# Two causal convolutions read TensorE's products in PSUM instead of a copy in SBUF

## The chip, the cores and the metric

The kernel runs on one core of a Trainium2 chip. The metric is the device time of one execution in microseconds (us). Five engines work side by side, each on a queue of its own instructions: TensorE (PE in the profile; PEld are its weight loads), VectorE (DVE), ScalarE (ACT), GpSimd (POOL) and SyncE (SP, which issues transfers). Matmuls write to PSUM, a memory of eight banks of 512 float32 columns in 128 partitions; the other engines read it, and SBUF holds everything else.

## What is computed

One step of one layer of a hybrid decoder, for a prompt of 2048 rows and for 8 sample sequences of 8 rows, with 1024 columns. The lines that matter here, cut from the reference:

```python
def causal_dwconv(x, buf, w):          # x (B,T,C), buf the W-1 rows before, w (W,C)
    width = w.shape[0]
    xp = jnp.concatenate([buf.astype(x.dtype), x], axis=1)
    y = xp[:, 0:t] * w[0]
    for j in range(1, width):
        y = y + xp[:, j:j + t] * w[j]
    return y, xp[:, t:]
...
z = hn @ w_in[i]
qkv, buf_qkv = causal_dwconv(z_qkv, conv_qkv[i], dn_conv_w[i])     # 4 taps, 1536 columns
qkv = jax.nn.silu(qkv).reshape(bsz, t, 3, DN_HEADS, DN_HEAD_DIM)
...                                   # delta rule, S5 and HGRN2 recurrences, output projection
up, buf_ffn = causal_dwconv(hn @ ffn_w_up[i], conv_ffn[i], ffn_conv_w[i])   # 3 taps, 5632 columns
a_ff, b_ff = jnp.split(up, 2, axis=-1)
h = h + (jax.nn.silu(a_ff) * b_ff) @ ffn_w_down[i]
```

So each convolved value is the sum of the products of its own row and of the 3 (or 2) rows before it. The rows before the first are zeros for the prompt and a given state for each sample. The last 3 (or 2) raw rows are outputs.

## The kernel before

**Layout.** The projections are computed transposed: the 128 columns of one weight block stand in the partitions, the rows of the input in the free dimension. The rows are cut into four groups. Groups 0 to 2 have 512 prompt rows each, group 3 has 512 prompt rows and the 64 sample rows, which it computes as two blocks of 320 and 256. Everything is float32 by splitting: an operand is a high part and the rest, and `mm3` issues three matmuls (high by high, high by low, low by high) for each of the 8 slices of 128 input columns, 24 matmuls to a block.

**Phases.** Phase 1 (line 832) is the input projection. It runs over the blocks of `p1_blocks` (line 769: two each of `hq`, `hg`, `u`, `hf`, then the twelve of `qkv`, then four of `zg`), a first pass with groups 0 and 1 and a second pass with groups 2 and 3. Between its blocks stand the small matmuls of the recurrences (delta rule, S5, HGRN2). Phase 3 is the output projection, phase 4 (line 2320) the up-projection over 44 blocks of 128 columns, again first groups 0 and 1, then 2 and 3. Phase 5 is the down-projection, and phase 6 the rest. In this execution the first pass of phase 1 lies at some 160 to 480 us, the second at 480 to 960, and the second pass of phase 4 at 1930 to 2420.

**PSUM.** The blocks of the projections go to the pool `mm` with three banks (line 2696), the small matmuls to the pool `mx` with five (line 2697). A bank can be written again when its last reader is done.

**A convolution unit** is one block of columns of one group. `p1_evac` (line 947) and `p4_evac` (line 2348) make it in these steps. `edges` (line 901, GpSimd) writes the 3 (or 2) columns ahead of the group into the SBUF tile `raw`: zeros, or the tail of the group before (`tail`, `ftail`), and in group 3 the samples' state (`stq`, `fst`) too. `conv_evac` (line 918, ScalarE) reads the bank twice, once unscaled to `raw` and once, scaled by the last tap's weight, to `y`; in group 3 a third copy takes the sample columns apart. From then on the bank is free. `conv` (line 927, VectorE) adds the other taps: for each, one `scalar_tensor_tensor` of 512 columns from `raw`, shifted by a column each time, into `y`, and in group 3 one of 64 sample columns. `keep` (line 937, GpSimd) copies the last columns of `raw` to the tail or, in group 3, to the output tiles `cso` and `fso`. ScalarE then applies silu, and `y` is stored to HBM (in phase 4 after a product with its pair).

**What sets the order.** The program is written once, in the order in which the Python code calls the engines, and each engine runs its instructions in that order. Steps after a matmul are put off: `later(ap, fn, ticks)` (line 787) queues a step, and `tick` (line 773), which the code calls after each slice of a block, issues it when a model (`Pace`, line 44) says that `ap` is ready, or after so many ticks at the latest. `Pace` adds up the modelled durations of each engine; it also knows a port that VectorE and GpSimd share, which operands in PSUM don't use. `tick` then lets the recurrences, which are generators, issue a step whose operands the model calls ready; `late` (line 426) holds them back while the model's queue of VectorE or ScalarE is over 2 us ahead. Weights are split in the background: ScalarE rounds the high part `wh`, and `split` (line 380) gives the subtraction that makes `wl` to VectorE or to GpSimd, whichever the model says is free earlier, with a handicap. So whatever a step costs in the model moves the instructions after it.

All instructions pass through one recording helper, so nearly all rows of the profile say line 71. They are told apart by the names of the tiles.

Of the kernel before, what the change touches and what calls it, by code (L numbers as in the profile page):

```python
# [9 lines left out]
F32 = mybir.dt.float32  # L10
# [9 lines left out]
DM = 1024  # L20
# [461 lines left out]
class Model:  # L482
# [418 lines left out]
    def edges(self, raw, taps, first, tail, rows):  # L901


        nc = self.nc
        k = taps - 1
        if first:
            nc.gpsimd.memset(raw[:, 0:k], 0.0)
        else:
            nc.gpsimd.tensor_copy(raw[:, 0:k], tail)
        if rows is not None:  # L910
            nc.gpsimd.tensor_copy(self.sample_part(raw, taps)[:, :, 0:k], rows)

    @staticmethod
    def sample_part(raw, taps):
        k = taps - 1
        return raw[:, k + 512:k + 512 + NSEQ * (k + ST)].rearrange("p (s t) -> p s t", t=k + ST)

    def conv_evac(self, raw, y, ps, c1, m, taps, w):

        k = taps - 1  # L920
        mp = min(m, 512 - c1)
        self.copy_act(raw[:, k + c1:k + c1 + mp], ps[:, :mp])
        self.copy_act(y[:, c1:c1 + m], ps[:, :m], w[:, k:k + 1])
        if mp < m:
            self.copy_act(self.sample_part(raw, taps)[:, :, k:], ps[:, mp:m].rearrange("p (s t) -> p s t", t=8))

    def conv(self, y, raw, w, taps, n):

        for j in range(taps - 1):
            self.nc.vector.scalar_tensor_tensor(y[:, :512], raw[:, j:j + 512], w[:, j:j + 1], y[:, :512], op0=OP.mult,  # L930
                                                op1=OP.add)
        if n > 512:
            ys, rs = y[:, 512:].rearrange("p (s t) -> p s t", t=8), self.sample_part(raw, taps)
            for j in range(taps - 1):
                self.nc.vector.scalar_tensor_tensor(ys, rs[:, :, j:j + 8], w[:, j:j + 1], ys, op0=OP.mult, op1=OP.add)

    def keep(self, raw, taps, last, tail, out):

        nc = self.nc
        k = taps - 1  # L940
        if last:
            nc.gpsimd.tensor_copy(out[:, 0:k], raw[:, 512:512 + k])
            nc.gpsimd.tensor_copy(out[:, k:].rearrange("p (s t) -> p s t", t=k), self.sample_part(raw, taps)[:, :, 8:])
        else:
            nc.gpsimd.tensor_copy(tail, raw[:, 512:512 + k])
# [1942 lines left out]
```

## Time and profile before

| what | value |
|---|---|
| time, median of 3 runs | 3195.06 us (3188.07 to 3197.48) |
| the profiled execution's own time | 3197.95 us |
| its span in the trace | 3196.2 us |
| mean granted clock of TensorE | 0.983 of full speed |
| TensorE busy | 3057.1 us, 96% |
| VectorE busy | 1893.4 us, 59% |
| ScalarE busy | 1195.7 us, 37% |
| GpSimd busy | 887.5 us, 28% |

The rows further down come from the profile page and from views of the same trace. A group of instructions has one row: line, engine, operation, the output tile, an arrow and the input tiles, the shape (partitions by columns), the number of instructions, their busy time and mean in ns, and then the time that the engine stood idle just ahead of them, with what ended most of it. The waits name who waited, for which engine's instruction on which tile, the time in all, how often, and the longest. The granted clock (PEclk) is TensorE's clock as the throttle gave it, as a share of full speed.

### The profile page before, as it was taken

Reading aid. Unit: us, or ns where it says so; the run is one execution under the profiler, and the core shown is the slowest. Engines: PE = TensorE matmul, PEld = TensorE weight load, DVE = VectorE, ACT = ScalarE, POOL = GpSimd, SP = SyncE. Lnnn points to the kernel's source line nnn. Section 1 sums busy time; section 2 is a strip of 40 time slices with the busy share of each in tenths; the row PEclk is TensorE's granted clock in tenths of the full one; section 3 lists DMA queues with packets and bytes.
Section 4 is the critical chain, followed back from the end, with each engine's and each line's share of the span. In section 5 each row is a group of like instructions: output and inputs, shape, how many; then the busy total and the mean of one; then the engine's idle time right before and its main releaser. Section 6 shows DMA issues by size and latency. Waiting matters only on the chain.

```text
span 3196.2 us, 49509 instructions
## 1 busy us (share of the span) xinstructions
PE 3057.1 (96%) x17872; PEld 2533.0 (79%) x17872; DVE 1893.4 (59%) x4208; ACT 1195.7 (37%) x2821; POOL 887.5 (28%) x1303
## 2 busy tenths in 40 slices
PE   6999989999998799999999999999999999999998
PEld 5767778878886677777777889998998888888886
DVE  8566975579696676777555456445444324323655
ACT  5343453443442444433324334333333213223332
POOL 3332423434243232533244225233231001000111
PEclk8999999999999899999999999999999999999999
DMA  6433496453656555344534333222216445444221
GB/s 187 110 112 93 123 261 170 121 155 85 195 148 200 154 160 143 120 118 133 132 89 115 114 108 116 65 71 72 65 51 190 131 124 169 132 134 131 80 79 57
DMA packets 576845, 400.32 MB, mean 125 GB/s; under 512 B 111077, under 2 KB 503145, under 8 KB 576328
## 3 DMA queue, kind: packets, MB, share of 16 engines
q1 hardware_dynamic: 545656, 359.07, 39.8%
q10 hardware_dynamic: 30944, 38.09, 3.4%
q8 instruction: 141, 2.31, 0.3%
q14 instruction: 104, 0.85, 0.1%
HBM read 277.52 MB, written 118.95 MB: 124 GB/s over the span
## 4 chain that ended last, share of the span: by engine, by line
PE 72%; DVE 15%; issue 4%; DMA 3%; ACT 3%; POOL 2%; SPq 1%; ACTq 0%; POOLq 0%; DVEq 0%
PE mm L71 61%; PE mx L71 11%; DVE y L71 3%; DVE rs L71 3%; DVE b L71 2%; DVE s5v L71 1%; DVE R L71 1%; SPq L71 1%; DVE dsc L71 1%; ACT djunk L71 1%; POOL wl L71 1%; ACT y L71 1%; DVE nx L71 0%; DMA Q<-dNN 0%; DMA h<-h 0%
## 5 line engine op out<-in xcount | busy, mean ns | idle before, releaser
L71 PE MATMUL mm<-hnl,wh 128*128 128x512 f32 (+2 forms) x2720 | 985.1, 362 | 8.8 <-DVE hnl L71 8.8
L71 PE MATMUL mm<-hnh,wl 128*128 128x512 f32 (+2 forms) x2720 | 980.6, 360 | 0.0
L71 PE MATMUL mm<-hnh,wh 128*128 128x512 f32 (+2 forms) x2720 | 978.7, 360 | 1.9 <-ACT y L71 1.6
L71 DVE SCALAR_TENSOR_TENSOR y<-raw,fw,y 128x512 f32<-128x512 f32 (+1 forms) x440 | 387.3, 888 | 395.1 <-ACT y L71 290.5
L71 PEld LDWEIGHTS mm<-hnl,wh 128*128 128x128 f32 x2720 | 516.1, 190 | 83.6 <-DVE hnl L71 9.3
L71 PEld LDWEIGHTS mm<-hnh,wh 128*128 128x128 f32 x2720 | 515.8, 190 | 76.9 <-issue 4.9
L71 PEld LDWEIGHTS mm<-hnh,wl 128*128 128x128 f32 x2720 | 516.2, 190 | 72.3 <-issue 3.0
L71 POOL TENSOR_TENSOR wl<-wr,wh 128x512 fp32r<-128x512 f32 (+1 forms) x291 | 410.9, 1420 | 519.6 <-ACT wh L71 466.0
L71 ACT ACTIVATE raw<-mm 128x512 f32<-128x512 f32 (+3 forms) x336 | 155.5, 463 | 415.3 <-PE mm L71 399.9
L71 PE MATMUL mm<-kh,ghi 128*128 128x512 f32 x748 | 294.7, 394 | 0.3 <-ACT ghi L71 0.3
L71 PE MATMUL mm<-kl,ghi 128*128 128x512 f32 x748 | 294.1, 393 | 0.0
L71 PE MATMUL mm<-kh,glo 128*128 128x512 f32 x704 | 277.1, 394 | 0.0
L71 ACT ACTIVATE wh<-wr 128x512 fp32r<-128x512 f32 (+1 forms) x338 | 204.3, 632 | 116.5 <-PE mm L71 53.2
L71 ACT ACTIVATE y<-y 128x512 f32<-128x512 f32 (+1 forms) x136 | 87.8, 645 | 367.6 <-DVE y L71 367.4
L71 ACT ACTIVATE ghi<-kr 128x512 fp32r<-128x512 f32 (+1 forms) x192 | 99.0, 580 | 329.7 <-PE mm L71 281.9
L71 DVE SCALAR_TENSOR_TENSOR y<-raw,cw,y 128x512 f32<-128x512 f32 (+1 forms) x180 | 156.2, 873 | 62.1 <-ACT y L71 28.3
L71 DVE TENSOR_TENSOR h<-mm,h 128x512 f32<-128x512 f32 (+1 forms) x36 | 24.8, 690 | 278.1 <-PE mm L71 278.0
L71 PEld LDWEIGHTS mm<-kh,ghi 128*128 128x128 f32 x748 | 140.6, 188 | 32.5 <-ACT ghi L71 0.7
L71 PEld LDWEIGHTS mm<-kl,ghi 128*128 128x128 f32 x748 | 140.6, 188 | 32.2 <-DVE kl L71 0.6
L71 POOL COPY ftail<-raw 128x2 f32<-128x2 f32 x132 | 31.5, 238 | 468.0 <-ACT raw L71 461.2
L71 PEld LDWEIGHTS mm<-kh,glo 128*128 128x128 f32 x704 | 132.2, 188 | 30.0 <-DVE glo L71 0.4
L71 ACT ACTIVATE y<-mm,fw 128x512 f32<-128x512 f32 (+2 forms) x220 | 133.7, 608 | 12.9 <-DVE y L71 12.0
(525 smaller groups left out, 4691.3 us busy)
## 6 DMA issues: line engine op xcount, KB each, us to landing
wr<-in_ffn_w_up SPq DMA_DIRECT2D x176, 256.0 KB
kr<-gT SPq DMA_DIRECT2D x155, 256.0 KB
wr<-in_w_in SPq DMA_DIRECT2D x112, 256.0 KB
gT<-y SPq DMA_DIRECT2D x66, 256.0 KB
h<-h SPq DMA_DIRECT2D x65, 256.0 KB
Q<-zq SPq DMA_DIRECT2D x32, 512.0 KB
wr<-oT SPq DMA_DIRECT2D x48, 256.0 KB
kr<-in_ffn_w_down SPq DMA_DIRECT2D x44, 256.0 KB
```

The source lines that it names most:

```text
L71: return f(*a, **k)
```

## The change

The tile `raw` is gone, and with it `edges`, `conv` and `keep`. ScalarE still writes `y`, scaled by the last tap, and then copies only the last 3 (or 2) columns of the bank, as the tail for the group behind; that tail has two slots now, by the parity of the group. In group 3 the tail between its two blocks goes to a small tile `ct`, and the last columns of the prompt and of each sample go straight to `cso` or `fso`. VectorE adds the other taps from the bank itself, block by block, so that group 3 has adds of some 318 and some 190 columns and of the samples' 5 to 7 rows out of eight. The first columns of a block lack the rows ahead of it; short adds from the tail (or the state) repair them. The conv step is put off by 9 ticks in phase 1 and 6 in phase 4. Two other users of `raw`'s memory take tiles `nx` instead (the fourth pair of phase 3, the state rows in `ffn_state`). The matmuls, their number and the pools of PSUM are as before.

```diff
@@ conv_evac, conv, keep, edges
-    def edges(self, raw, taps, first, tail, rows):
...
-        nc = self.nc
-        k = taps - 1
-        if first:
-            nc.gpsimd.memset(raw[:, 0:k], 0.0)
-        else:
-            nc.gpsimd.tensor_copy(raw[:, 0:k], tail)
-        if rows is not None:
-            nc.gpsimd.tensor_copy(self.sample_part(raw, taps)[:, :, 0:k], rows)
...
+    def conv_evac(self, y, ps, c1, m, taps, w, tail, rows, last, out):
...
         k = taps - 1
         mp = min(m, 512 - c1)
-        self.copy_act(raw[:, k + c1:k + c1 + mp], ps[:, :mp])
         self.copy_act(y[:, c1:c1 + m], ps[:, :m], w[:, k:k + 1])
+        self.copy_act(out[:, 0:k], ps[:, mp - k:mp])
         if mp < m:
-            self.copy_act(self.sample_part(raw, taps)[:, :, k:], ps[:, mp:m].rearrange("p (s t) -> p s t", t=8))
-
-    def conv(self, y, raw, w, taps, n):
-
-        for j in range(taps - 1):
-            self.nc.vector.scalar_tensor_tensor(y[:, :512], raw[:, j:j + 512], w[:, j:j + 1], y[:, :512], op0=OP.mult,
-                                                op1=OP.add)
...
-    def keep(self, raw, taps, last, tail, out):
...
+            self.copy_act(out[:, k:].rearrange("p (s t) -> p s t", t=k), self.by_seq(ps[:, mp:m])[:, :, ST - k:])
+
+        def add(o, i, j):
+            nc.vector.scalar_tensor_tensor(o, i, w[:, j:j + 1], o, op0=OP.mult, op1=OP.add)
+
+        def conv():
+            for j in range(k):
+                add(y[:, c1 + k - j:c1 + mp], ps[:, :mp - k + j], j)
+            if mp < m:
+                ys, xs = self.by_seq(y[:, 512:512 + NS]), self.by_seq(ps[:, mp:m])
+                for j in range(k):
+                    add(ys[:, :, k - j:], xs[:, :, :ST - k + j], j)
+                for j in range(k):
+                    add(ys[:, :, :k - j], rows[:, :, j:], j)
+            if tail is not None:
+                for j in range(k):
+                    add(y[:, c1:c1 + k - j], tail[:, j:k], j)
+
+        return conv
+
+    def conv_block(self, y, ps, c1, m, n, taps, w, g, tail, rows, out):
+
+        last = c1 + m == n
+        if c1 == 0:
+            self.before = None if g == 0 else tail[:, (g - 1) % 2]
+        to = (out if g == 3 else tail[:, g % 2]) if last else self.sm.tile([128, 3], F32, tag="ct", name="ct")
+        conv = self.conv_evac(y, ps, c1, m, taps, w, self.before, rows, last, to)
+        self.before = to
+        return conv
 
@@ p1_evac
-            if kind == "qkv":
-                self.raw = self.cv.tile([128, 3 + 512 + NSEQ * 11], F32, tag="raw", name="raw")
-                self.edges(self.raw, 4, g == 0, self.tail[:, b],
-                           self.stq[:, b].rearrange("p (s t) -> p s t", t=3) if g == 3 else None)
...
-            self.conv_evac(self.raw, y, ps, c1, m, 4, self.cw[:, b])
+            conv = self.conv_block(y, ps, c1, m, n, 4, self.cw[:, b], g, self.tail[:, b],
+                                   self.stq[:, b].rearrange("p (s t) -> p s t", t=3), self.cso[:, b])
+
+            def rest():
+                conv()
+                if c1 + m == n:
+                    self.p1_finish(g, kind, b, y)
+
+            self.later(y, rest, 9)
+            return
...
-            self.later(self.raw, conv, 12)
+            self.later(y, silu, 9)
@@ phase3, pair
-            if t < 2:
+            if t != 2:
                 return halves(self.np_.tile([128, DM], F32, tag="nx", name="h1x", bufs=self.NX))
-            if t == 2:
-                self.h1y = i
-            return tuple(y_tile() if t == 2 else half_tile("raw", 3 + 512 + NSEQ * 11, 2) for _ in range(2))
+            self.h1y = i
+            return y_tile(), y_tile()
@@ ffn_consts, ffn_state, and the same for tail in phase 1
-        self.ftail = cp.tile([128, 44, 2], F32, name="ftail")
+        self.ftail = cp.tile([128, 44, 2, 2], F32, name="ftail")
...
-            sr = self.cv.tile([128, 3 + 512 + NSEQ * 11], F32, tag="raw", name="fs_rows")[:16, :512]
+            sr = self.np_.tile([128, DM], F32, tag="nx", name="fs_rows", bufs=self.NX)[:16, :512]
@@ p4_evac
-            self.raw = self.cv.tile([128, 3 + 512 + NSEQ * 11], F32, tag="raw", name="raw")
...
-        raw, y = self.raw, self.y
-        self.conv_evac(raw, y, ps, c1, m, 3, self.fw[:, b])
+        y = self.y
+        block = self.conv_block(y, ps, c1, m, n, 3, self.fw[:, b], g, self.ftail[:, b],
+                                self.fst[:, b].rearrange("p (s t) -> p s t", t=2) if g == 3 else None,
+                                self.fso[:, b] if g == 3 else None)
...
-            self.conv(y, raw, self.fw[:, b], 3, n)
-            self.keep(raw, 3, g == 3, self.ftail[:, b], self.fso[:, b] if g == 3 else None)
+            block()
+            if c1 + m < n:
+                return
...
-        if c1 + m == n:
-            self.later(raw, conv, 9)
+        self.later(y, conv, 6)
```

The step that is put off moves the instructions behind it. Three places follow, without the numbers of the rows. In them `y<-mm,cw,y` is an add out of the bank with a weight of the convolution, `s5t`, `s5v`, `la` and `lbm` belong to the S5 scan, `hw`, `hm` to HGRN2, `R` and `V` to the delta rule; a number behind a name is a buffer's.

VectorE in the first pass of phase 1, the end of a run of serial S5 steps and the convolution unit behind it, before:

```order
L71 TENSOR_TENSOR s5t<-b_3025,lbm 128x16
L71 TENSOR_TENSOR b_3025<-s5v,s5t 128x16
L71 TENSOR_TENSOR b_3025<-b_3025,s5t 128x8 x2
L71 SCALAR_TENSOR_TENSOR y<-raw,cw,y 128x512 x3
L71 TENSOR_TENSOR s5t<-b_3025,la 128x16
```

and after:

```order
L71 TENSOR_TENSOR s5t<-b_2992,lbm 128x16
L71 TENSOR_TENSOR b_2992<-s5v,s5t 128x16
L71 TENSOR_TENSOR b_2992<-b_2992,s5t 128x8 x2
L71 SCALAR_TENSOR_TENSOR y<-mm,cw,y 128x509
L71 SCALAR_TENSOR_TENSOR y<-mm,cw,y 128x510
L71 SCALAR_TENSOR_TENSOR y<-mm,cw,y 128x511
L71 SCALAR_TENSOR_TENSOR y<-tail,cw,y 128x3
L71 SCALAR_TENSOR_TENSOR y<-tail,cw,y 128x2
L71 SCALAR_TENSOR_TENSOR y<-tail,cw,y 128x1
L71 TENSOR_TENSOR s5t<-b_2992,la 128x16
```

Eight S5 steps of five instructions stand ahead of the adds in both orders; the adds are now six instead of three, and read the bank.

VectorE in the second pass of phase 1, a unit of group 3 (the delta rule's and HGRN2's instructions around it), before:

```order
L71 TENSOR_TENSOR hw<-hw,b_7920 128x8x32
L71 COPY_PREDICATED b_7919<-hm,mx 32x4x32 x4
L71 SCALAR_TENSOR_TENSOR y<-raw,cw,y 128x512 x3
L71 SCALAR_TENSOR_TENSOR y<-raw,cw,y 128x64 x3
L71 SCALAR_TENSOR_TENSOR R_8667<-mx,d_neg,V 128x128 x4
```

and after, the second of its two blocks:

```order
L71 SCALAR_TENSOR_TENSOR y<-mm,cw,y 128x189
L71 SCALAR_TENSOR_TENSOR y<-mm,cw,y 128x190
L71 SCALAR_TENSOR_TENSOR y<-mm,cw,y 128x191
L71 SCALAR_TENSOR_TENSOR y<-mm,cw,y 128x8x5
L71 SCALAR_TENSOR_TENSOR y<-mm,cw,y 128x8x6
L71 SCALAR_TENSOR_TENSOR y<-mm,cw,y 128x8x7
L71 SCALAR_TENSOR_TENSOR y<-stq,cw,y 128x8x3
L71 SCALAR_TENSOR_TENSOR y<-stq,cw,y 128x8x2
L71 SCALAR_TENSOR_TENSOR y<-stq,cw,y 128x8
L71 SCALAR_TENSOR_TENSOR y<-ct,cw,y 128x3
L71 SCALAR_TENSOR_TENSOR y<-ct,cw,y 128x2
L71 SCALAR_TENSOR_TENSOR y<-ct,cw,y 128x1
```

Six adds of the unit are now eighteen: these twelve, and ahead of them six of the first block (317 to 319 columns, and the repairs of 3, 2 and 1).

GpSimd at the end of phase 1 (`SQ` belongs to the delta rule), before:

```order
L71 TENSOR_TENSOR wl<-wr,wh 128x512 x2
L71 TENSOR_TENSOR SQ<-O,ofac 128x512
L71 COPY raw<-tail 128x3
L71 COPY raw<-stq 128x8x3
L71 COPY cso<-raw 128x3
L71 COPY cso<-raw 128x24
L71 TENSOR_TENSOR wl<-wr,wh 128x512
```

and after:

```order
L71 TENSOR_TENSOR b_9025<-b_8875,hfac 128x512
L71 TENSOR_TENSOR wl<-wr,wh 128x512
L71 TENSOR_TENSOR SQ<-O,ofac 128x512
L71 TENSOR_TENSOR wl<-wr,wh 128x512 x2
L71 TENSOR_TENSOR SQ<-O,ofac 128x512
```

The copies into and out of `raw` are gone, and the splits `wl` stand closer together. Over the whole program `wl` splits of 512 columns go from 44 to 9 on VectorE and from 276 to 311 on GpSimd.

## Rows read from the trace of the kernel before

**Rows 1.** The page, part 1: engine, busy us, share of the span, instructions.
```profile
PE 3057.1 (96%) x17872; PEld 2533.0 (79%) x17872; DVE 1893.4 (59%) x4208; ACT 1195.7 (37%) x2821; POOL 887.5 (28%) x1303
```

**Rows 2.** Busy time by stretches; the first line names the columns.
```profile
core 0: us, PE busy (x) PEld busy (x) DVE busy (x) ACT busy (x) POOL busy (x), PEclk, DMA share, GB/s
...
160.00:480.00 320.00, 294.18 (x1859) 236.33 (x1858) 240.67 (x617) 143.64 (x343) 102.47 (x138) 0.97 0.50 147
480.00:960.00 480.00, 454.92 (x3872) 394.83 (x3870) 346.83 (x889) 204.36 (x580) 180.37 (x223) 0.97 0.52 145
960.00:1100.00 140.00, 110.73 (x493) 87.94 (x494) 99.64 (x249) 46.34 (x123) 47.59 (x38) 0.91 0.60 180
1100.00:1600.00 500.00, 479.48 (x3060) 379.52 (x3060) 343.97 (x794) 208.81 (x546) 168.11 (x275) 0.98 0.49 135
...
1930.00:2420.00 490.00, 490.00 (x2991) 446.58 (x2990) 241.74 (x318) 187.12 (x419) 159.71 (x313) 1.00 0.23 71
```

**Rows 3.** TensorE's waits, 160 to 1600 us: waiter, releaser, us, times, longest.
```profile
PE mx L71 <- DVE d_g L71: 15.3, 4, 6.0
...
PE mx L71 <- POOL raw L71: 5.1, 3, 3.4
...
PE mm L71 <- ACT y L71: 3.8, 2, 2.3
...
PE mx L71 <- POOL A L71: 0.3, 1, 0.3
```

**Rows 4.** ScalarE: costliest groups (busy, mean ns, idle before); a tile's instructions (min/median/max).
```profile
L71 ACT ACTIVATE raw<-mm 128x512 f32<-128x512 f32 (+3 forms) x336 | 155.5, 463 | 415.3 <-PE mm L71 399.9
...
L71 ACT ACTIVATE ba<-mm x17: 158/172/188, 25.2 to 952.0; 128x8 f32<-128x8 f32 x16, 64x8 f32<-64x8 f32 x1
```

**Rows 5.** Groups of GpSimd and VectorE, each shape apart; columns as there.
```profile
L71 POOL TENSOR_TENSOR wl<-wr,wh 128x512 fp32r<-128x512 f32 x276 | 390.3, 1422 | 465.5 <-ACT wh L71 430.1 <-DMA b<-xs 15.9 <-ACT d_egc L71 11.3
...
L71 POOL COPY ftail<-raw 128x2 f32<-128x2 f32 x132 | 31.5, 238 | 468.0 <-ACT raw L71 461.2 <-DVE R L71 3.0 <-DMA A<-dA 2.0
...
L71 DVE TENSOR_TENSOR wl<-wr,wh 128x512 fp32r<-128x512 f32 x44 | 32.4, 737 | 13.5 <-ACT wh L71 13.3 <-issue 0.2
```

**Rows 6.** Groups of VectorE: two of the page, then four with shapes apart.
```profile
L71 DVE SCALAR_TENSOR_TENSOR y<-raw,fw,y 128x512 f32<-128x512 f32 (+1 forms) x440 | 387.3, 888 | 395.1 <-ACT y L71 290.5
...
L71 DVE SCALAR_TENSOR_TENSOR y<-raw,cw,y 128x512 f32<-128x512 f32 (+1 forms) x180 | 156.2, 873 | 62.1 <-ACT y L71 28.3
...
L71 DVE SCALAR_TENSOR_TENSOR SH<-SH,b,mx 64x64 f32<-64x64 f32 x128 | 35.8, 279 | 29.3 <-PE mx L71 26.1
...
L71 DVE SCALAR_TENSOR_TENSOR R<-mx,d_neg,V 128x128 f32<-128x128 f32 x64 | 18.0, 343 | 26.8 <-PE mx L71 26.8
...
L71 DVE SCALAR_TENSOR_TENSOR ZG<-mx,gdn,ZG 128x512 f32<-128x512 f32 x16 | 12.0, 748 | 17.3 <-PE mx L71 14.0 <-DMA A<-dA 3.3
...
L71 DVE SCALAR_TENSOR_TENSOR nrs<-rs 128x1 f32<-128x1 f32 x64 | 10.2, 160 | 2.2
```

**Rows 7.** One group of VectorE, shapes apart, in 480 to 960 us.
```profile
L71 DVE SCALAR_TENSOR_TENSOR y<-raw,cw,y 128x512 f32<-128x512 f32 x72 | 72.2, 1003 | 17.2 <-POOL raw L71 4.7 <-ACT y L71 4.2 <-POOL tail L71 3.4
```

**Rows 8.** The instructions of the tiles `raw` and `hnh`: min/median/max ns, from when, shapes.
```profile
L71 DVE SCALAR_TENSOR_TENSOR y<-raw,fw,y x440: 271/752/3448, 1100.0 to 2421.2; 128x512 f32<-128x512 f32 x104, 128x64 f32<-128x64 f32 x43
...
L71 DVE TENSOR_TENSOR hnl<-mx,hnh x68: 416/683/692, 16.4 to 1909.1; 128x512 fp32r<-128x512 f32 x64, 128x256 fp32r<-128x256 f32 x4
```

**Rows 9.** VectorE's waits, 160 to 1600 us, columns as in Rows 3.
```profile
DVE y L71 <- ACT y L71: 67.2, 27, 9.2
...
DVE y L71 <- POOL ftail L71: 29.7, 8, 9.4
...
DVE y L71 <- POOL raw L71: 18.4, 9, 3.6
```

**Rows 10.** Start and length, us: the chain that ended last; timelines of ScalarE, VectorE.
```profile
1668.76 39.97 PE mm L71 x171
...
343.16 0.60 ACT L71 ACTIVATE raw<-mm 128x512 f32<-128x512 f32 x1 [0.46 <-ACT y L71]
...
354.75 2.32 DVE L71 SCALAR_TENSOR_TENSOR y<-raw,cw,y 128x512 f32<-128x512 f32 x3
```

More of the change, by code (lines that the diff above doesn't have):

```diff
@@ L927, in conv @@
-    def conv(self, y, raw, w, taps, n):
-        for j in range(taps - 1):
-            self.nc.vector.scalar_tensor_tensor(y[:, :512], raw[:, j:j + 512], w[:, j:j + 1], y[:, :512], op0=OP.mult,
-                                                op1=OP.add)
[L932 to L935, printed above, removed]
@@ L937, in keep @@
-    def keep(self, raw, taps, last, tail, out):
-        nc = self.nc
[L940 to L945, printed above, removed]
+            self.copy_act(out[:, k:].rearrange("p (s t) -> p s t", t=k), self.by_seq(ps[:, mp:m])[:, :, ST - k:])
+        def add(o, i, j):
+            nc.vector.scalar_tensor_tensor(o, i, w[:, j:j + 1], o, op0=OP.mult, op1=OP.add)
@@ L987, in out @@
             self.flags.add((kind, b, g))
-        def conv(raw=self.raw if kind == "qkv" else None):
-            self.conv(y, raw, self.cw[:, b], 4, n)
-            self.keep(raw, 4, g == 3, self.tail[:, b], self.cso[:, b])
-            self.later(y, silu, 9)
         def silu():
@@ L2210, in phase3 @@
         both = units[0][0] == units[1][0]
[L2211 to L2212 removed]
+        y_tile = lambda: self.cv.tile([128, 512 + NS], F32, tag="y", name="xh", bufs=3)[:, :512]
         turn = 3 if both else 4
@@ L2355, in p4_evac @@
                 self.need(("hn2", self.h1y))
-            self.raw = self.cv.tile([128, 3 + 512 + NSEQ * 11], F32, tag="raw", name="raw")
             self.y = self.cv.tile([128, 512 + NS], F32, tag="y", name="y", bufs=3)
-            self.edges(self.raw, 3, g == 0, self.ftail[:, b],
-                       self.fst[:, b].rearrange("p (s t) -> p s t", t=2) if g == 3 else None)
-        raw, y = self.raw, self.y
-        self.conv_evac(raw, y, ps, c1, m, 3, self.fw[:, b])
+        y = self.y
+        block = self.conv_block(y, ps, c1, m, n, 3, self.fw[:, b], g, self.ftail[:, b],
+                                self.fst[:, b].rearrange("p (s t) -> p s t", t=2) if g == 3 else None,
+                                self.fso[:, b] if g == 3 else None)
         def conv():
-            self.conv(y, raw, self.fw[:, b], 3, n)
-            self.keep(raw, 3, g == 3, self.ftail[:, b], self.fso[:, b] if g == 3 else None)
+            block()
+            if c1 + m < n:
+                return
             if x == 0:
@@ L2619, in setup_small @@
         self.stq = cp.tile([128, 12, 24], F32, name="stq")
-        self.tail = cp.tile([128, 12, 3], F32, name="tail")
+        self.tail = cp.tile([128, 12, 2, 3], F32, name="tail")
         self.cso = self.cp.tile([128, 12, 27], F32, name="cso")
```

10 lines of the change are left out of this document (3 added, 7 removed).

## Prediction, made before the changed kernel ran

> **What bounds the kernel now.** I read the page's busy times first. TensorE is busy for 96% of the span [rows 1], so an edit that issues no matmul can only pay where TensorE waits. The table by stretches tells where that is. From 1930 to 2420 us, the second pass of the up-projection, TensorE is busy for 490.00 of 490 us at a granted clock of 1.00. It waits in the first half: 25.82 us idle from 160 to 480, 25.08 from 480 to 960, 29.27 from 960 to 1100, 20.52 from 1100 to 1600. That is 100.7 us of 1440, with a granted clock of 0.97, 0.97, 0.91 and 0.98 [rows 2]. If a clock of 0.91 means that 9% of the stretch's matmul rate is missing, the clock costs up to 47 us more there (9.6 + 14.4 + 12.6 + 10.0).
>
> The waits of TensorE in 160 to 1600 us say for whom. There are 25 rows, the first and the last shown, and they add up to 100.6 us: 45.1 for VectorE, 21.3 for ScalarE, 13.2 for GpSimd, 21.0 for transfers. Nearly all are `mx`, the small matmuls of the recurrences that stand in TensorE's order between the blocks of the projection. The projection itself (`mm`) waits for a bank only for 3.8 us [rows 3]. So the convolution is not on the path now. It matters in two ways: it occupies the queues of VectorE, ScalarE and GpSimd that feed the small matmuls, and after the change it also holds the bank.
>
> **The change, part by part.** The program lists the same 15,709 matmuls and transposes before and after. The small ones stand a few blocks earlier or later, and I cost that at nothing by itself.
>
> ScalarE. The 336 copies `raw<-mm` go, 155.5 us. In their place come 280 copies of 2 or 3 columns and 56 of 16 or 24. The nearest row is the 128x8 copy `ba<-mm` at 0.172 us [rows 4], so 336 x 0.172 = 58 us; if each cost what a whole `raw<-mm` costs (0.463), nothing would be gained. I take 58: 97 us off a queue of 1195.7 us, all of it beside matmuls.
>
> GpSimd. All 504 copies into and out of `raw` go; at the mean of the cheapest of their rows, 0.238, that is 120 us. Against that, 35 weight splits `wl` of 512 columns go from VectorE to GpSimd in the new order (44 to 9, and 276 to 311): 35 x 1.422 = 50 us more there and 35 x 0.737 = 26 us less on VectorE [rows 5]. GpSimd ends some 70 us lighter.
>
> VectorE. Removed: 387.3 + 156.2 = 543.5 us. Added are 372 adds of about 510 columns out of PSUM, 124 of about 318, 124 of about 190, 124 of 40 to 56 for the samples, and 620 of one to 24 columns out of SBUF, which repair the first columns. The row with just the operands of the large ones (PSUM, a scalar by partition, SBUF) is `ZG<-mx,gdn,ZG`, 0.748 for 512 columns; `R<-mx,d_neg,V` has 0.343 for 128. The line between them gives 0.543 for 318 and 0.408 for 190; the samples cost about `SH<-SH,b,mx`, 0.279 for 64. A repair lies between `nrs<-rs`, 0.160 for one column, and 0.279, and I take 0.20, nearer to the first [rows 6]. The sum is 372 x 0.748 + 124 x (0.543 + 0.408 + 0.279) + 620 x 0.20 = 278 + 153 + 124 = 555 us (530 to 604). With the splits that left, VectorE changes by 555 - 543.5 - 26 = -14 us (-39 to +35).
>
> It is unevenly spread. A unit is one block of 128 output columns over one group of rows. In 480 to 960 us, where the last group brings the samples along, the twelve pairs of units cost 72.2 us for the 512-column adds and 36 x 0.279 = 10 for the samples before, and 36 x 0.748 + 36 x (0.543 + 0.408 + 0.279) + 144 x 0.20 = 100 us after: +18 us on 346.83 that VectorE is busy there [rows 2, 7]. In 1100 to 1600 us, where the first groups have no or two repairs, it falls.
>
> What goes besides is waiting. An add out of `raw` takes 0.752 us as a rule and up to 3.448 while GpSimd works; the subtraction `hnl<-mx,hnh`, which reads PSUM, stays between 0.416 and 0.692 over 68 instructions [rows 8]. So the large adds lose their tail (mean 0.888 and 0.873 over all forms), and the repairs, with SBUF on both sides, keep one. VectorE's 48.1 us of waiting for GpSimd's `ftail` and `raw` copies (29.7 + 18.4) in 160 to 1600 us goes altogether [rows 9].
>
> On the path: TensorE's 5.1 us of waiting for GpSimd's `raw` copies goes. VectorE's queue gets shorter by about 48 of the 1031 us that it is busy in 160 to 1600, 5%; I take 5% off the other 74.5 us that TensorE waits for the three engines, 4 us. Together -9 us. After 1600 us there is nothing to gain, and I take 0 (0 to +5).
>
> The added wait. A bank of `mm` now comes free after VectorE's last add instead of ScalarE's second copy, and there are three such banks. What is queued behind a late one is the next-but-two block of matmuls, so TensorE itself. A block of 24 matmuls of 512 columns takes 24 x 39.97 / 171 = 5.6 us, so the adds must end 11.2 us after the block. Three adds at 0.752 are 2.3 us, so a unit that meets an empty queue is far inside. The worst is in a row: ScalarE reads the bank at 343.16, and the three adds stand behind the serial S5 steps until 354.75 + 2.32 = 357.07 us, 13.9 us later [rows 10]. In the new order the adds of such a unit still stand behind eight of these steps. I take 3 us for this one and nothing for the rest.
>
> The Trainium skill speaks against this change. "VectorE: DVE Perf Modes", in its rules for kernel authors, says to accept the plain rate out of PSUM or to copy to SBUF first if many operations follow, and its errata section puts the fixed part at 120 cycles out of PSUM against 58. At the page's 0.96 GHz that would be an estimated 65 ns for each of 744 adds, 48 us more on VectorE; that would take back the 4 us of its shorter queue, and the sum below would be 3194 instead of 3190. The rows disagree: 0.748 out of PSUM and a median of 0.752 out of SBUF [rows 6, 8].
>
> The sum: the profiled execution took 3197.95 us (span 3196.2); 3197.95 - 9 + 3 = 3192. The median of the three runs shown, 3195.06, lies 2.9 lower, so I forecast 3190.
>
> **The rivals.** *The queues pay more.* VectorE alone waited 67.2 us for ScalarE's `y` in 160 to 1600 us [rows 9], and the raw copy that stood ahead of each `y` is gone. If a third of the 79.6 us that TensorE waits for the three engines goes, that is 27 us and 3168. For it: 97 and 70 us leave the two side queues. Against it: a chain of small matmuls waits for its own last step, whatever the load.
>
> *The banks decide: slower.* Place: 480 to 960 us, where a block of 512 is followed by one of 320 and one of 256 columns, 576 x 5.6 / 512 = 6.3 us for both, and where VectorE gets 18 us more to do. There an add chain that ends over 6.3 us after its block stops TensorE. If the backlog grows by 3 us in each of the twelve units, about half of that shows: 12 x 1.5 = 18, with 5 us in the first pass 23 us, so 3213. It decides from the point where adds end later than two blocks after their own. For it: 343 to 357 us shows 14 us behind an end of a block. Against it: 3.8 us of bank waits now, and the planner keeps its recurrences back when VectorE is more than 2 us behind.
>
> *The change doesn't do what it says.* GpSimd's freed time goes into the 35 splits, and the wait for ScalarE only moves: 3195.
>
> **How the numbers follow.** About 0.3% (9.6 us) is what a measurement of this kernel can tell from no change. The forecast gets 0.38 and the last rival 0.07, both within it but for 0.03 below; the queues pay more 0.31; the banks 0.24, of which 0.01 stays within. So faster 0.34, same 0.43, slower 0.23. The range 3166 to 3214 reaches to the middle of both rivals on the outside, 3168 and 3213, which leaves about 0.1 out on each side.
>
> **What would show it.** No `raw` row; ScalarE near 1100 and GpSimd near 810 us busy; the 510-column adds at 0.75 with no tail. TensorE busy throughout from 1930 to 2420. Its waits for `DVE y` at `mm` stay under 10 us in all: if they pass 20, the banks decided. If the idle of TensorE from 160 to 1600 falls under 80 us, the queues paid more. I am wrong altogether if the time after 1600 us moves by more than 5 us.

## The result, and the profile after

The changed kernel takes 3215.04 us (median of 5 runs, 3207.5 to 3222.19) against 3195.06 us before. The ratio is 1.0062, with a 95% interval of 1.0045 to 1.0078. So it is slower, by about 20 us, and above the range that I gave (3166 to 3214). The profiled execution took 3215.56 us, its span is 3213.8.

The busy times of the changed kernel, to be read beside [rows 1]:

```profile
PE 3066.5 (95%) x17872; PEld 2539.5 (79%) x17872; DVE 1958.6 (61%) x4911; ACT 1093.2 (34%) x2818; POOL 755.8 (24%) x784
```

ScalarE fell by 102.5 us and GpSimd by 131.7, both more than forecast. VectorE did not fall by 14 us; it rose by 65.2.

The stretches of [rows 2], after, with the same columns:

```profile
160.00:480.00 320.00, 290.63 (x1835) 233.91 (x1834) 240.30 (x653) 130.02 (x334) 91.65 (x95) 0.97 0.49 143
480.00:960.00 480.00, 446.77 (x3773) 386.19 (x3771) 337.93 (x944) 177.50 (x544) 136.53 (x143) 0.96 0.49 138
960.00:1100.00 140.00, 117.18 (x544) 95.12 (x543) 112.06 (x318) 51.54 (x133) 56.68 (x43) 0.91 0.55 167
1100.00:1600.00 500.00, 480.89 (x3080) 380.68 (x3078) 346.69 (x891) 189.54 (x571) 141.69 (x152) 0.98 0.50 141
...
1930.00:2420.00 490.00, 489.60 (x2973) 445.36 (x2972) 304.18 (x713) 152.81 (x424) 112.73 (x88) 1.00 0.23 72
```

In 480 to 960 us TensorE is busy for 446.77 us instead of 454.92. In the second pass of the up-projection it is as full as before, although VectorE works 62 us more there (304.18 against 241.74). That work is covered.

A fixed point of the program shows when the time is lost. The first matmul of the output projection (`mm<-woh,wh`) follows phase 1, the first of the down-projection (`mm<-kh,ghi`) follows phase 4. The instructions of the tiles, before and then after (min/median/max ns, first and last start in us):

```profile
L71 PE MATMUL mm<-woh,wh x128: 388/394/793, 951.5 to 1078.9; 128*128 128x512 f32 x128
L71 PE MATMUL mm<-kh,ghi x748: 387/392/497, 2417.3 to 2932.4; 128*128 128x512 f32 x187
```

```profile
L71 PE MATMUL mm<-woh,wh x128: 387/394/775, 969.5 to 1098.8; 128*128 128x512 f32 x128
L71 PE MATMUL mm<-kh,ghi x748: 387/392/639, 2429.1 to 2947.6; 128*128 128x512 f32 x187
```

The output projection begins 18.0 us later. By the down-projection 6.2 of them are back, and 5.8 more are lost behind it, 17.6 in all.

Cut at these two points, the program shows what the 17.6 us are made of (columns as in [rows 2], before and then after):

```profile
0.00:951.50 951.50, 874.62 (x6333) 734.32 (x6334) 689.91 (x1806) 409.10 (x1036) 331.69 (x439) 0.97 0.51 146
951.50:2417.30 1465.80, 1415.18 (x8111) 1177.93 (x8110) 867.32 (x1663) 563.62 (x1318) 489.92 (x813) 0.98 0.39 112
2417.30:3196.20 778.90, 767.26 (x3432) 620.77 (x3430) 336.19 (x741) 222.96 (x467) 65.94 (x51) 1.00 0.43 125
```

```profile
0.00:969.50 969.50, 879.32 (x6314) 737.14 (x6315) 698.03 (x1954) 381.44 (x1016) 284.96 (x320) 0.96 0.50 143
969.50:2429.10 1459.60, 1417.77 (x8132) 1180.46 (x8131) 927.34 (x2215) 489.18 (x1336) 403.59 (x414) 0.98 0.38 113
2429.10:3213.80 784.70, 769.45 (x3432) 621.90 (x3430) 333.22 (x744) 222.63 (x467) 67.29 (x50) 0.99 0.41 124
```

TensorE issues the same 17872 instructions. It is idle for 8.2 us more (147.3 against 139.1) and busy for 9.4 us more. So only half of the loss is waiting; the other half is the same matmuls at a lower granted clock, 0.980 over the whole span instead of 0.983, and 0.003 of 3214 us is 9.6. Up to the output projection it is 13.3 us of idle time and 4.7 of busy time.

### The profile page after: what moved, and what is told of

It is laid out like the page before. It is cut to its first block, busy times and chain, and to the rows that moved or that the text cites. A ratio compares the mean times of both kernels' runs of the same rounds, so it can differ in the third digit from the quotient of the medians.

```text
span 3213.8 us, 49643 instructions
## 1 busy us (share of the span) xinstructions
PE 3066.5 (95%) x17872; PEld 2539.5 (79%) x17872; DVE 1958.6 (61%) x4911; ACT 1093.2 (34%) x2818; POOL 755.8 (24%) x784
## 4 chain that ended last, share of the span: by engine, by line
PE 57%; DVE 13%; DMA 4%; issue 3%; ACT 1%; POOL 1%; SPq 0%; ACTq 0%; POOLq 0%; DVEq 0%
PE mm L71 49%; PE mx L71 7%; DVE y L71 4%; DVE R L71 3%; DVE rs L71 1%; DVE b L71 1%; DMA h<-h 1%; DVE s5v L71 1%; DMA wr<-oT 1%; DVE dsc L71 0%; DMA t<-dTU 0%; SPq L71 0%; ACT y L71 0%; DMA Q<-dNN 0%; DMA b<-us 0%
## 5 line engine op out<-in xcount | busy, mean ns | idle before, releaser
L71 POOL TENSOR_TENSOR wl<-wr,wh 128x512 fp32r<-128x512 f32 (+1 forms) x327 | 430.7, 1331 | 1205.9 <-ACT wh L71 1138.9
L71 DVE SCALAR_TENSOR_TENSOR y<-mm,fw,y 128x510 f32<-128x510 f32 (+7 forms) x528 | 302.3, 579 | 306.6 <-ACT ftail L71 222.1
L71 DVE SCALAR_TENSOR_TENSOR y<-mm,cw,y 128x511 f32<-128x511 f32 (+8 forms) x216 | 123.9, 578 | 43.5 <-ACT tail L71 31.7
L71 POOL TENSOR_TENSOR kl<-kr,kh 128x512 fp32r<-128x512 f32 x12 | 16.7, 1398 | 449.6 <-ACT kh L71 440.3
L71 PE MATMUL mx<-b,b 64*64 64x64 f32 (+7 forms) x752 | 108.5, 290 | 11.3 <-DMA b<-us 7.9
```

What stands on the lines that cost most here:

```text
L71: return f(*a, **k)
```

## What VectorE did in place of the forecast

VectorE's groups in the changed kernel, each shape apart (count, busy us, mean ns, idle before):

```profile
L71 DVE SCALAR_TENSOR_TENSOR y<-mm,fw,y 128x510 f32<-128x510 f32 x132 | 98.5, 747 | 224.6 <-ACT ftail L71 222.1 <-DMA gT<-y 2.3
...
L71 DVE SCALAR_TENSOR_TENSOR y<-ftail,fw,y 128x1 f32<-128x1 f32 x132 | 55.6, 421 | 4.7
...
L71 DVE SCALAR_TENSOR_TENSOR y<-fst,fw,y 128x8 f32<-128x8 f32 x44 | 29.1, 662 | 1.6
...
L71 DVE SCALAR_TENSOR_TENSOR y<-ct,fw,y 128x2 f32<-128x2 f32 x44 | 9.3, 212 | 0.0
```

The large adds cost just what the sum took: 0.747 us, 278 us for the 372. The middle ones and the samples' come to 153 us, as forecast. The 620 repairs cost 227 us instead of 124, a mean of 0.366 instead of 0.20. By itself that would have made VectorE 89 us busier (103 - 14); some of its other instructions became shorter, such as the product `y<-y` of 512 columns, 0.704 us instead of 0.822. The repairs' median is low, but there is a tail (the tile `ftail`, changed kernel):

```profile
L71 DVE SCALAR_TENSOR_TENSOR y<-ftail,fw,y x264: 219/221/2357, 1154.5 to 2428.6; 128x2 f32<-128x2 f32 x132
```

A place in the second pass of phase 1 shows where the tail is from. VectorE's timeline, and GpSimd's for the same time (start, length in us):

```profile
787.21 0.73 DVE L71 SCALAR_TENSOR_TENSOR y<-tail,cw,y 128x3 f32<-128x3 f32 x3
787.86 2.09 DVE L71 SCALAR_TENSOR_TENSOR y<-mm,cw,y 128x189 f32<-128x189 f32 x6
789.98 1.32 DVE L71 SCALAR_TENSOR_TENSOR y<-stq,cw,y 128x24 f32<-128x24 f32 x3
791.23 1.15 DVE L71 SCALAR_TENSOR_TENSOR y<-ct,cw,y 128x3 f32<-128x3 f32 x3
792.29 0.91 DVE L71 TENSOR_TENSOR R<-Q,R 128x392 f32<-128x392 f32 x1
```

```profile
790.42 0.85 POOL L71 TENSOR_TENSOR hw<-hw 128x256 f32<-128x256 f32 x1 [3.98 <-PE mx L71]
791.24 0.61 POOL L71 TENSOR_TENSOR b<-hw 128x256 f32<-128x256 f32 x1
```

Three repairs take 0.73 us while GpSimd is idle, and 1.32 and 1.15 while it works. Over the whole trace, the 188 repairs that overlap a busy GpSimd instruction of over 0.1 us have a mean of 0.70 us, and the 432 others 0.22, at most 0.245. The Trainium skill ("SBUF — State Buffer", Terms) calls this the shared port pair, held for the full instruction, on which the loser fully blocks. The rows agree: the three repairs from `stq` end at 791.30 us, GpSimd's first instruction at 791.27.

Around this place VectorE is the path. The chain of waits of the changed kernel in 730 to 830 us, by line; below it the same line of the kernel before:

```profile
by line: DVE y L71 56.4%; DVE R L71 21.1%; issue 11.2%; DVE hw L71 2.5%; ACT y L71 2.3%; DVE b L71 2.0%; DVE rs L71 1.7%; DVE SH L71 1.1%; ACT Q L71 1.1%; ACT tail L71 0.6%; DVE hfac L71 0.2%; ACTq L71 0.1%; DVEq L71 0.1%
```

```profile
by line: PE mm L71 27.6%; DVE y L71 21.1%; PE mx L71 17.9%; DVE R L71 8.3%; issue 7.3%; DVE rs L71 3.4%; ACT y L71 2.9%; DVE hw L71 2.4%; ACT raw L71 2.2%; DMA zq<-y 2.1%; POOL wl L71 1.3%; ACT Q L71 1.2%; POOL cso L71 0.7%; ACT wh L71 0.5%
```

TensorE's matmuls had 46% of it (27.6 + 17.9) and have none. And TensorE now waits for VectorE at the bank (three of its waits in 160 to 1600 us; all of them add up to 104.0 us against 100.6 before):

```profile
PE mx L71 <- DVE d_g L71: 15.4, 3, 11.3
PE mm L71 <- DVE y L71: 14.9, 8, 4.4
PE mx L71 <- DVE b L71: 7.9, 3, 5.5
```

Of these 14.9 us, 9.8 lie between 740 and 815 us, where blocks of 320 and 256 columns follow each other. Two stretches with their clocks (columns as in [rows 2]), before and then after:

```profile
740.00:815.00 75.00, 68.48 (x597) 59.73 (x596) 67.56 (x120) 26.93 (x63) 36.70 (x53) 0.95 0.43 120
815.00:860.00 45.00, 44.53 (x411) 38.30 (x409) 26.30 (x81) 20.96 (x78) 7.73 (x12) 1.00 0.68 196
```

```profile
740.00:815.00 75.00, 65.17 (x425) 57.81 (x424) 66.40 (x162) 18.13 (x49) 17.72 (x17) 0.95 0.27 84
815.00:860.00 45.00, 38.82 (x355) 31.10 (x353) 26.83 (x77) 13.58 (x37) 9.59 (x14) 0.84 0.57 159
```

VectorE was already busy for 90% of 740 to 815 us before the change. TensorE is idle for 9.8 us there now (6.5 before), and in the 45 us that follow its granted clock is 0.84, between its two levels (1.00 is 2.4 GHz, 0.50 is 1.2 GHz), where it was 1.00.

## The experiments

Three theories stood against each other. *Repairs*: their 227 us lengthen VectorE's queue, and the small matmuls of the recurrences wait behind it. *Banks*: TensorE waits for a bank that VectorE still reads. *Order*: the recurrences stand in other places, and 35 splits moved to GpSimd; that costs it. All ratios are against the kernel before on the same chip, with 95% intervals.

**Order and work apart.** In x_order the planning model notes the changed kernel's instructions (`nc.note`), while the engines get those of the kernel before (`real`):

```diff
+        nc.note(nc.scalar, "activation", (out[:, 0:k], ps[:, mp - k:mp], AF.Copy), {})
...
+            nc.note(nc.vector, "scalar_tensor_tensor", (o, i, w[:, j:j + 1], o), {})
...
+        act, dve, pool = nc.scalar.real, nc.vector.real, nc.gpsimd.real
...
+        act.activation(raw[:, k + c1:k + c1 + mp], ps[:, :mp], AF.Copy)
...
+                dve.scalar_tensor_tensor(y[:, :512], raw[:, j:j + 512], w[:, j:j + 1], y[:, :512], op0=OP.mult, op1=OP.add)
```

> The convolution is made as in the kernel before (raw copies on ScalarE, adds out of SBUF, edges and keeps on GpSimd), but the model that sets the order is fed the changed kernel's instructions, so that TensorE's order, the places of the steps and the engine of each weight split are those of the changed kernel. Theory 'order' (the recurrences' new places and the 35 moved splits cost the 20 us): 3211 to 3220. Theories 'banks' and 'repairs' (the work itself costs it): 3190 to 3200, the time of the kernel before.

Measured: 3213.54 us, ratio 1.0047 (1.0029 to 1.0065). This is what "order" expected. But it is an order that was planned for other work, so it may be the mismatch that costs 15 us and not the order by itself. And the place differs (the two fixed points in x_order):

```profile
L71 PE MATMUL mm<-woh,wh x128: 388/394/762, 958.0 to 1085.6; 128*128 128x512 f32 x128
L71 PE MATMUL mm<-kh,ghi x748: 387/392/505, 2434.3 to 2950.0; 128*128 128x512 f32 x187
```

Its output projection begins 6.5 us late, where the changed kernel is 18.0 late; it loses another 10.5 by the down-projection, where the changed kernel gains 6.2. So the two times are alike, but the losses are not the same: of the 18.0 us in phase 1, this run shows 6.5 without the new work.

**The bank let go early.** x_sbuf:

```diff
+        nc.scalar.real.activation(raw[:, c1:c1 + mp], ps[:, :mp], AF.Copy)
...
-                add(y[:, c1 + k - j:c1 + mp], ps[:, :mp - k + j], j)
+                add_raw(y[:, c1 + k - j:c1 + mp], ps[:, :mp - k + j], raw[:, c1:c1 + mp - k + j], j)
```

> The changed kernel in its own order, with the same adds and repairs on VectorE, except that ScalarE copies each bank to SBUF as well and the large adds read that copy: a bank is free as soon as ScalarE is done. Theory 'banks': TensorE's 15 us of waiting for VectorE's adds at a bank go, 3198 to 3203. Theory 'repairs' (VectorE's longer queue delays the recurrences): nothing comes back, 3213 or more, since VectorE's work is the same and its large adds now share the port with GpSimd. Theory 'order': 3213 to 3220.

Measured: 3286.22 us, ratio 1.0285 (1.0261 to 1.0308). No theory named a loss of that size; "repairs" had only said 3213 or more. The adds out of SBUF have their tail again (the second large add of the up-projection takes 1.064 us instead of 0.750), and the repairs come on top. The bank waits did not go either, they changed their releaser (TensorE's waits, 160 to 1600 us):

```profile
PE mm L71 <- ACT tail L71: 14.8, 5, 4.2
```

So this run does not tell the bank from the queue. It does price the choice that the prediction cited from the Trainium skill ("VectorE: DVE Perf Modes", rules for kernel authors), to accept the plain rate out of PSUM or to copy to SBUF first if many operations follow. In this order, with two or three adds behind it, copying first costs 71 us against reading PSUM.

**The repairs left out.** In x_norepair `skip` notes a repair in the planning model and does not issue it:

```diff
-                    add(y[:, c1:c1 + k - j], tail[:, j:k], j)
+                    skip(y[:, c1:c1 + k - j], tail[:, j:k], j)
```

> The changed kernel in its own order without the 620 short adds that repair the first columns of each block; these columns of the convolutions lack the rows ahead of the block. VectorE should lose their 227 us. Theory 'repairs': 3193 to 3200. Theory 'banks': the adds end up to 1 us earlier in each unit, so only some of the 15 us of waiting at the banks goes, 3203 to 3211. Theory 'order': 3211 to 3220.

Measured: 3168.31 us, ratio 0.9914 (0.99 to 0.9929). That is below the range of every theory: the repairs cost 47 us, more than the whole loss, and all the rest of the change, the new order with it, is worth -27 us. In the stretch with most of the bank waits TensorE is full now, and the chain of waits in 730 to 830 us is TensorE's again:

```profile
740.00:815.00 75.00, 75.00 (x622) 67.13 (x622) 61.95 (x128) 26.86 (x69) 25.23 (x27) 1.00 0.46 129
by line: PE mm L71 76.6%; PE mx L71 14.3%; DVE R L71 3.8%; DVE y L71 3.2%; DVE rs L71 1.7%; issue 0.8%; DVE hfac L71 0.2%
```

The two kernels stand in one plan, so their matmuls can be compared one by one. By the profiled executions the changed kernel is 2.1 us behind at 700 us of its time, 34.0 at 880, 39.9 at 1600 and 43.4 near the end. So 32 us arise within 180, in which 108 repairs take 29 us of VectorE. The 56 repairs in 1100 to 1600 us take 27.5 and cost 4.5. The stretch 700 to 880 us with its clock, the changed kernel and then x_norepair:

```profile
700.00:880.00 180.00, 162.42 (x1173) 137.90 (x1172) 142.25 (x420) 55.45 (x182) 34.84 (x41) 0.91 0.34 98
700.00:880.00 180.00, 179.25 (x1488) 155.09 (x1487) 130.94 (x361) 68.46 (x224) 42.88 (x46) 1.00 0.52 145
```

**One half of the change.** p1_only has the new code in `p1_evac` alone, p4_only in `p4_evac` alone.

> Only the convolution of the input projection (qkv, 4 taps) reads PSUM; that of the up-projection is as before. Theory 'banks': nearly all of the 15 us of bank waits lie before 960 us, in phase 1, so 3207 to 3214. Theory 'repairs': 180 of the 620 repairs and 61 of their 227 us are here, so about a quarter to a half of the 20 us, 3200 to 3205. Theory 'order': cannot say, since this order is a third one.

> Only the convolution of the up-projection reads PSUM; that of the input projection is as before. The other half alone gave +13 us. If the halves add up, 3200 to 3205. Theory 'banks': hardly any bank wait lies after 960 us, so 3190 to 3198. Theory 'repairs': of the up-projection's 440 repairs only 56 run before 1600 us, a quarter of the 236 there, so +2 to +5 against the gain of the adds out of PSUM, 3190 to 3200.

Measured: p1_only 3208.69 us, 1.004 (1.0027 to 1.0054); p4_only 3189.09 us, 0.9989 (0.998 to 0.9999). The up-projection's half gains 4 us, the input projection's loses 13. p1_only lies within the range of "banks" and above that of "repairs", p4_only 1 us below both. They add up to +9 and not to +20, so the halves act on each other, or some 10 us hang on the order. In phase 1 they do add up: the output projection begins at 972.4 us in p1_only and at 950.4 in p4_only, 20.9 late and 1.1 early, and 18.0 late with both. What does not add up lies behind it.

**The plan told the true price.** v_model:

```diff
+        if op == "scalar_tensor_tensor" and n <= 24 and outs[0].tensor.name[:2] == "y_":
+            return 0.37
```

> The changed kernel with one number of the planning model altered: an add of at most 24 columns is taken to cost 0.37 us on VectorE (measured mean) instead of some 0.16 to 0.18. Work and matmuls are the same; the planner holds background steps back longer. If the loss comes from an order planned on repairs that are too cheap: 3195 to 3207. If it comes from the repairs' time itself: 3210 to 3220.

Measured: 3214.76 us, 1.0069 (1.0055 to 1.0082). Planning with the right price gives nothing back, so the loss does not come from a plan that took the repairs for too cheap.

**Fewer repairs on VectorE.** v_fold sums the samples' state times the weights once; v_act makes the other repairs on ScalarE as well:

```diff
-                for j in range(k):
-                    add(ys[:, :, :k - j], rows[:, :, j:], j)
+                nc.vector.tensor_add(ys[:, :, :k], ys[:, :, :k], rows)
...
+                    nc.scalar.activation(o, tail[:, c + d:c + d + 1], AF.Identity, bias=o, scale=w[:, d:d + 1])
```

> The changed kernel with only the 124 repairs from the samples' state folded into 56 adds, as in v_act. VectorE should lose some 45 us, nearly all of it after 1930 us, where TensorE does not wait for it, and 8 us in the second pass of phase 1. Theory 'repairs': 3208 to 3214. Theory 'order': anything within 10 us of 3215.

> The changed kernel with the 496 repairs from `tail`, `ftail` and `ct` moved to ScalarE (one column an instruction, 816 of them, just ahead of silu or of the gate's product, when the bank is long free), and the 124 repairs from the samples' state folded: GpSimd sums state times weights once, and VectorE adds the sum with one instruction a unit. VectorE should lose some 205 us, ScalarE gain 816 x 0.165 = 135 us. Theory 'repairs' (they cost 47 us in the run without them): 3165 to 3190, faster than the kernel before. Theory 'order' (the new order alone costs 15 us): 3205 to 3220, as the order is again another one that nothing was tuned for.

Measured: v_fold 3219.73 us, 1.0085 (1.007 to 1.0101), above what "repairs" expected and within what "order" allowed; v_act 3189.53 us, 0.9987 (0.9977 to 0.9996). v_fold shortened VectorE's work by 7 us, not 45. Part of the wait for GpSimd moved to the next instruction with both operands in SBUF: the first repair from `ct` took 0.212 us in the changed kernel and takes 0.712 here:

```profile
L71 DVE SCALAR_TENSOR_TENSOR y<-ct,fw,y 128x2 f32<-128x2 f32 x44 | 31.3, 712 | 0.0
```

v_act gives 25 of the 47 us back. ScalarE's repairs turned out dear, 0.383 us each instead of 0.165:

```profile
L71 ACT ACTIVATE y<-ftail,y,fw 128x1 f32<-128x1 f32 x396 | 132.8, 383 | 89.6 <-DVE y L71 89.6
```

**The same repairs without the port.** In x_rep_psum `mend` notes the repair as it was and issues one that reads the bank:

```diff
-                    add(y[:, c1:c1 + k - j], tail[:, j:k], j)
+                    mend(y[:, c1:c1 + k - j], tail[:, j:k], j, ps[:, :k - j])
```

> The changed kernel in its own order with all 620 repairs, but each takes its columns from the bank instead of the tail or the state in SBUF (so the first columns of a block are wrong). Work, order and bank are the same; only the share in the SBUF port with GpSimd is gone from the repairs. If a repair costs 0.366 us because of GpSimd, it should now take 0.22, and VectorE's queue be 90 us shorter: 3193 to 3205. If the wait for GpSimd only moves to the next instruction that works in SBUF alone: 3208 to 3216, with VectorE's total nearly as before.

Measured: 3205.11 us, 1.0037 (1.0024 to 1.005). The repairs now take 0.219 us and VectorE 1896.5 us in all, close to the forecast of the sum:

```profile
L922 DVE SCALAR_TENSOR_TENSOR y<-mm,fw,y 128x1 f32<-128x1 f32 x176 | 38.5, 219 | 6.2
```

So the wrong price of a repair is worth 8 to 10 us, give or take 7, nearly half of the loss. At the price that I had taken, the kernel would still have been slower. The run changes one thing more: its repairs also hold the bank longer. In the profiled execution, which took 3217.94 us, TensorE waits 16.0 us at banks, in two rows, instead of 14.9. So the port may be worth somewhat more.

```profile
PE mm L71 <- DVE y L922: 9.9, 6, 3.2
PE mm L71 <- DVE y L71: 6.1, 3, 4.4
```

**A fourth bank.** a_bank44 and b_bank44 split the eight banks four and four; n_bank44 leaves the repairs out as well:

```diff
-    m.mmp = ctx.enter_context(pool("mmp", 3, space=PSUM))
-    m.mx = ctx.enter_context(pool("mxp", 5, space=PSUM))
+    m.mmp = ctx.enter_context(pool("mmp", 4, space=PSUM))
+    m.mx = ctx.enter_context(pool("mxp", 4, space=PSUM))
```

> The changed kernel with four banks for the projections and four for the small matmuls instead of three and five (so the order is planned anew). Theory 'banks': TensorE's 15 us of waiting for VectorE's adds go under 3 us, and the time falls by 10 to 15 against the same split made in the kernel before (b_bank44). Theory 'repairs': the difference to b_bank44 stays at 15 to 25 us.

> The kernel before with four banks for the projections and four for the small matmuls: the control for a_bank44. The projections waited 3.8 us for a bank, the recurrences lose one of five: 3195 to 3240 by all theories.

> The changed kernel with four and four banks, in the order of a_bank44 (3202), without the 620 repairs (the first columns of each block lack the rows ahead of it). With three banks taking the repairs away gave back 47 us. If the repairs cost TensorE its time only through the bank, which they keep VectorE from letting go in time, little comes back here, where TensorE no longer waits for a bank: 3192 to 3204. If they cost it through VectorE's queue, behind which the recurrences' steps stand, as much comes back as with three banks: 3155 to 3170.

Measured: a_bank44 3202.36 us, 1.0023 (1.0013 to 1.0033); b_bank44 3205.71 us, 1.0035 (1.0024 to 1.0046); n_bank44 3170.5 us, 0.9916 (0.9903 to 0.993). With four banks the change is not slower than its control. That is more than "banks" had said (10 to 15 us off the difference of 20, and it is 23), and against "repairs". n_bank44 lies at the range for the queue (3155 to 3170) and far from the one for the bank. The bank waits are gone, and TensorE is full in 740 to 815 us although VectorE is as busy there as in the changed kernel (a_bank44, a wait of TensorE in 160 to 1600 us and the stretch):

```profile
PE mm L71 <- DVE y L71: 0.4, 1, 0.4
740.00:815.00 75.00, 75.00 (x474) 66.60 (x474) 66.18 (x172) 25.14 (x77) 16.07 (x13) 1.00 0.37 102
```

| | with the repairs | without them | difference |
|---|---|---|---|
| three banks | +0.62% | -0.86% | 1.48%, 47 us |
| four banks | +0.23% | -0.84% | 1.07%, 34 us |

Where hardly any bank is waited for, the repairs still cost 34 us: through the queue. With three banks they cost 13 more, near the 14.9 us of bank waits, but the intervals leave 4 to 22. Without the repairs a fourth bank is worth nothing. So -27 + 34 + 13 = +20.

That the 13 us are the bank's is argued from these differences and not shown by the waits. Other waits came in place of those at the banks: TensorE's idle time over the whole span is 144.7 us in a_bank44 and 147.3 in the changed kernel. What fell is its busy time over the same matmuls, 3057.7 us against 3066.5, at a granted clock of 0.982 against 0.980. And the split itself costs the kernel before 11 us. Against that control the change with four banks is 3 us faster, which would put 23 us on the bank instead of 13. Which of the two comparisons is right stays open.

**A version that beats both.** v_spill lets the later adds run over a block's end into unused columns of `y`; a copy of these stands in for the tail, and the next block needs one short add, out of the bank:

```diff
+            if lead:
+                add(y[:, c1:c1 + k], ps[:, :k], k, before)
             for j in range(k):
-                add(y[:, c1 + k - j:c1 + mp], ps[:, :mp - k + j], j)
+                e = k - j if spill and j else 0
+                add(y[:, c1 + k - j:end + e], ps[:, :mp - k + j + e], j)
```

> The changed kernel with the repairs made otherwise. The later adds of a block run over its end and leave there what the next block's first columns lack, so that the next block needs one short add (its own product in the bank times the last tap, plus what was left) instead of two or three; the samples' state is folded once as in v_fold. All short adds, 280 instead of 620, read the bank. At some 0.2 us each VectorE does 56 us of them instead of 227; GpSimd saves what was left, 168 copies of 0.2 us. Theory 'repairs': near the run without repairs (3168) plus 10 to 15, 3170 to 3190. Theory 'order': 3200 to 3220. If the bank held longer by the short adds decides: 3210 or more.

> The variant v_spill (3184 with three banks, 11.9 us of TensorE's waiting for VectorE's adds at a bank) with four and four banks. If the bank costs it what it waits there: 3172 to 3180. If the small matmuls' fifth bank is worth as much, as in the kernel before (+11 us by the same step): 3183 to 3198.

Measured: v_spill 3183.68 us, ratio 0.9966 (0.9953 to 0.998), 11 us faster than the kernel before and 31 faster than the changed one. Its short adds cost 0.218 us and wait for no port:

```profile
L71 DVE SCALAR_TENSOR_TENSOR y<-mm,fw,ftail 128x2 f32<-128x2 f32 x132 | 28.8, 218 | 262.8 <-ACT y L71 257.4 <-POOL R L71 4.0 <-issue 1.4
```

With four banks (s_bank44) it takes 3184.72 us, 0.9964 (0.9951 to 0.9978): no difference, though it had waited 11.9 us at banks. That speaks against reading the bank waits as the price of the bank.

## Why the prediction was wrong

- *What bounds the kernel*: right in the large. TensorE has 489.60 of 490 us in the second up-projection pass, and the loss arises in phase 1. But a stretch of 480 us was too wide to see that VectorE is the limit inside it: 346.83 of 480 us is 72%, while 740 to 815 us stood at 90%.
- *ScalarE and GpSimd*: right in kind and low in size, -102.5 against -97 and -131.7 against -70. A split on GpSimd got cheaper, 1.325 us instead of 1.422.
- *VectorE*: the large adds, the middle ones and the samples' were exact (278 and 153 us). The repairs were mis-sized, 227 us against 124. I had [rows 8] with a tail of 3.448 us for adds out of SBUF, wrote that the repairs keep such a tail, and took the price from `nrs<-rs` [rows 6], which shows none. That is worth 8 to 10 us (x_rep_psum).
- *On the path*: this is the step that failed. -9 us was wrong on both sides. Without repairs the change is worth -27 us: x_norepair's time, 3168, is that of the rival "the queues pay more", and its sign came too, 75.3 us of idle time of TensorE from 160 to 1600. And the repairs cost 34 to 47 us; 236 of them, 83 us of VectorE's time, lie before 1600 us, so each microsecond of these cost 0.4 to 0.6 at the end, and in 700 to 880 us about one (32 us for 29). I had priced VectorE's queue by its share of TensorE's waits, 4 us for 48. These 48 us were time that VectorE waited, not work; for its work I had found 18 us more in 480 to 960 us, and that had no price in the sum.
- *The clock*: I had put up to 47 us on it in the first half of the kernel and then gave it no term, without a reason. TensorE's busy time over the same matmuls rose by 9.4 us, half of the loss.
- *The added wait*: I took 3 us, for a unit like the one at 343 to 357 us. No bank wait of over 1 us stands there in the changed kernel; there is one of 4.4 us at 167, and 9.8 us lie in the place that the rival "the banks decide" named, 14.9 in all. That is between its two marks, 10 and 20. The rival's time, 3213, was near, but by the runs its mechanism is some 13 of the 20 us, and it needs the repairs. Before the change the blocks had waited 7.6 us for copies out of their banks, not 3.8; one more stands in TensorE's waits under the tile `ba`:

```profile
PE mm L71 <- ACT ba L71: 3.8, 1, 3.8
```

- *After 1600 us*: the forecast was 0 to +5, and I said that over 5 would be wrong altogether. Behind the start of the down-projection 5.8 us are lost. TensorE is idle for 3.6 us more there and busy for 2.2 more over the same 3432 instructions. A wait of 2.0 us for `ghi` near its start is new (0.3 before), and the granted clock of the first 42.7 us is 0.96 instead of 1.00; why `ghi` came late is open.
- *"It doesn't do what it says"*: out; the work of ScalarE and GpSimd went as said.

Open stays how much the order by itself costs. x_order gives +15 for a mismatch of plan and work, 6.5 of it in phase 1, and the halves don't add up by 11 us; three other plans of about the same work (the changed kernel, v_model, v_fold) lie between 3215 and 3220. The runs without repairs also stand in an order planned with them, so 47 and 34 us may hold some of that. The 11 us that the split with four banks costs the kernel before don't show as waiting either: TensorE is idle for 135.6 us in b_bank44 against 139.1, and busy for 3071.8 against 3057.1, at a granted clock of 0.977.

## What to carry to other kernels

Look for the engine's share in stretches as short as the queue that it feeds; an average of 60% hides 75 us at 90%, and around there the short instructions counted in full here. Price the small repair instructions that an elegant edit brings with it by the row whose operands lie in the same memory and that runs beside the same neighbour. When a reader takes the place of a copy, the bank is held by that reader's whole queue. And split a loss into idle and busy time of the limiting engine: half of this one was TensorE's clock.

## What the runs showed of the hardware

- VectorE's instructions with one operand in PSUM are not slowed by GpSimd (0.219 us for a short add, at most 0.241 over 440 in x_rep_psum); the same with both in SBUF take 0.22 us alone and 0.70 beside it, at most 2.357.
- The wait for GpSimd falls on whichever instruction with both operands in SBUF meets it: of two repairs from `ftail` the second was the longer one (0.421 us against 0.314). Taking such instructions away can move the wait to the next (0.212 to 0.712 us in v_fold).
- TensorE's granted clock was 0.91 in 700 to 880 us, where the engine was idle for 17.6 us, and 1.00 in the same stretch without the repairs, where it was idle for 0.75.
- ScalarE's copy of two columns out of PSUM takes 0.163 us; one column in SBUF with a scale and a bias by partition takes 0.383.
